# Strided slice by DMA alone: one queue for loads, one for stores, and single-batch copies beside them

## The chip, the cores and the metric

The kernel runs on one core of a Trainium2 chip. The metric is the device time of one execution in microseconds. Times are medians of several executions. The profile is of one execution, and its span (first to last instruction) is about 1.8 us shorter than the time of that execution. "GB/s" counts bytes that the core's 16 DMA engines moved; a byte copied from HBM to HBM counts once there, though HBM reads it and writes it.

## The reference

```python
batch, seq, dim = 32, 1024, 512          # float32; start, stop, stride = 0, 512, 2
def reference(x, start, stop, stride):
    return x[:, start:stop:stride, :].astype(np.float32)
```

Of each batch, rows 0, 2, 4 ... 510 are kept: 256 rows of 2 KB, 4 KB apart in the input and adjacent in the output. The output has 16.78 MB.

## The kernel before

Nothing is computed, so the kernel is only transfers. It sends half of the rows of a batch straight from HBM to HBM (a copy, issued by GpSimd) and the other half through SBUF (a load, later a store). The halves are the even and the odd kept rows. `apart` tells which half of batch b is copied directly, and it changes every two batches.

```python
def apart(b):
    return 1 - (b >> 1 & 1)

def two(t, b, step, parity):             # one half of two batches, step apart
    return t[b : b + step + 1 : step].rearrange("b (p two) d -> two p b d", two=2)[parity]
...
    src = x[:, start:stop:stride, :]
    held = [io.tile([P, 2, D], x.dtype, name=f"held{i}") for i in range(B // 2)]
    for g in range(0, B, EIGHT):
        for i, (b, step) in enumerate(((0, 5), (2, 5), (1, 3), (3, 3))):
            b += g
            at = g + 2 * i
            (sp, act)[i % 2].dma_start(held[at // 2], two(src, at, 1, 1 - apart(at)))       # load
            pool.dma_start(two(out, b, step, apart(b)), two(src, b, step, apart(b)))        # copy
    for b in range(B):
        to = out[b].rearrange("(p two) d -> two p d", two=2)[1 - apart(b)]
        sp.dma_start(to, held[b // 2][:, b % 2])                                            # store
```

All 16 loads and 16 copies come first, and SyncE (SP) issues all the stores behind its loads. Every pair of batches has its own SBUF tile, so no buffer is ever waited for.

Of the kernel before, what the change touches and what calls it, by code (L numbers as in the profile page):

```python
# [3 lines left out]

EIGHT = 8


def apart(b):


    return 1 - (b >> 1 & 1)


def two(t, b, step, parity):

    return t[b : b + step + 1 : step].rearrange("b (p two) d -> two p b d", two=2)[parity]


def kernel(tc, x, start, stop, stride, out):





    nc = tc.nc
    src = x[:, start:stop:stride, :]
    B, rows, D = out.shape
    P = rows // 2
    sp, act, pool = nc.sync, nc.scalar, nc.gpsimd
    with tc.tile_pool(name="io", bufs=1) as io:  # L30
        held = [io.tile([P, 2, D], x.dtype, name=f"held{i}") for i in range(B // 2)]
        for g in range(0, B, EIGHT):
            for i, (b, step) in enumerate(((0, 5), (2, 5), (1, 3), (3, 3))):
                b += g
                at = g + 2 * i
                (sp, act)[i % 2].dma_start(held[at // 2], two(src, at, 1, 1 - apart(at)))
                pool.dma_start(two(out, b, step, apart(b)), two(src, b, step, apart(b)))  # L37
        for b in range(B):
            to = out[b].rearrange("(p two) d -> two p d", two=2)[1 - apart(b)]
            sp.dma_start(to, held[b // 2][:, b % 2])  # L40


# [1 line left out]
_INS = ['x', 'start', 'stop', 'stride']  # L44
_OUTS = [((32, 256, 512), 'float32')]

_NUMBERS = {'start': 0, 'stop': 512, 'stride': 2}


def kernel(**inputs):  # L50
    import numpy as _np
    import concourse.bacc as _bacc
    import concourse.tile as _tile
    from concourse import mybir as _mybir
    from concourse.bass_utils import run_bass_kernel_spmd as _run

    nc = _bacc.Bacc("TRN2", target_bir_lowering=False, num_devices=1)  # L57
    arrays, args = {}, []
    for name in _INS:
        if name in _NUMBERS:  # L60
            args.append(_NUMBERS[name])
            continue
        a = _np.ascontiguousarray(inputs[name])
        if a.dtype.kind in "iu":
            a = a.astype(_np.int64)
        arrays[f"in_{name}_dram"] = a
        args.append(nc.dram_tensor(f"in_{name}_dram", a.shape, _mybir.dt.from_np(a.dtype), kind="ExternalInput").ap())
    for i, (shape, dtype) in enumerate(_OUTS):
        dt = _mybir.dt.from_np(_np.dtype(dtype))
        args.append(nc.dram_tensor(f"out_{i}_dram", shape, dt, kind="ExternalOutput").ap())  # L70
    with _tile.TileContext(nc) as tc:  # L71
        kernel(tc, *args)
    r = _run(nc, [arrays], core_ids=[0])
    got = tuple(r.results[0][f"out_{i}_dram"] for i in range(len(_OUTS)))
    return got[0]
```

## Time and profile before

| What | Value | From |
|---|---|---|
| time | 79.45 us median of 3 (79.29 to 79.64) | the runs |
| the profiled execution | 79.17 us, span 77.4 us | its result, the page |
| loads, copies, stores | 8.39 MB each | the page's queue rows and issues |
| mean rate of the DMA engines | 325 GB/s | the page |
| rate of HBM, read and written | 434 GB/s over the span | the page |

The prediction below shows the lines behind this. A share of 1 means that the times of the packets add up to the time of all 16 engines (it reaches 1.06 here, as packets overlap a little). The rate can still differ, because a packet can be held up while it is in progress. The packet records of the trace give each packet's start, length, size and queue.

### The profile page before, as it was taken

To read this page: it belongs to the slowest core of one execution; us is meant where nothing else is said; L and a number is where in the kernel's file an instruction comes from. 1 tells how busy PE (TensorE), PEld (TensorE's weight loads), DVE (VectorE), ACT (ScalarE), POOL (GpSimd) and SP (SyncE) were. 2 spreads that over 40 slices of the span, in tenths; PEclk is the share of its full clock that TensorE was granted. 3 is DMA by queue.
4 is the path that set the end of the run, shared out by engine and by line. 5 is a ranking of instruction groups with operands and counts; after the bars stand their busy time and mean duration, and the time that the engine had idled before them with its cause. 6 is when DMAs were issued, how large, how long until landed. Compare 5 with 4: busy or idle time off the path is not lost. (4 is left out here: it accounts for less than half of the span.)

```text
span 77.4 us, 113 instructions
## 1 busy us (share of the span) xinstructions
POOL 11.3 (15%) x20
## 2 busy tenths in 40 slices
POOL 4995003303023031130000000000000000000000
DMA  0799999999999999999999999999999999999960
GB/s 7 235 303 334 332 281 347 327 310 386 351 349 363 364 314 358 358 321 333 323 300 310 347 307 357 413 392 339 402 404 405 375 356 347 361 356 353 350 216 20
DMA packets 11264, 25.17 MB, mean 325 GB/s; under 512 B 1024, under 2 KB 1024, under 8 KB 11264
## 3 DMA queue, kind: packets, MB, share of 16 engines
q1 hardware_dynamic: 6784, 12.59, 48.1%
q0 software_dynamic: 2304, 8.39, 29.3%
q10 hardware_dynamic: 2176, 4.19, 17.7%
HBM read 16.78 MB, written 16.78 MB: 434 GB/s over the span
## 5 line engine op out<-in xcount | busy, mean ns | idle before, releaser
L37 POOL DMA_DIRECT2D out_dram<-in_x_dram x16 | 11.1, 696 | 22.6 <-DMA out_dram<-in_x_dram 21.8
L57 POOL MEMSET const-float32-0.0<- 128x1 f32 x1 | 0.1, 99 | 0.2 <-issue 0.2
L57 POOL MEMSET const-bfloat16-1.0<- 128x1 bf16 x1 | 0.1, 102 | 0.0
L57 POOL MEMSET const-uint8-127<- 128x1 uint8 x1 | 0.1, 100 | 0.0
L57 POOL MEMSET const-float32-1.0<- 128x1 f32 x1 | 0.1, 99 | 0.0
## 6 DMA issues: line engine op xcount, KB each, us to landing
out_dram<-in_x_dram POOLq DMA_DIRECT2D x16, 512.0 KB, 23.6
out_dram<-held SPq DMA_DIRECT2D x32, 256.0 KB, 6.1
held<-in_x_dram ACTq DMA_DIRECT2D x8, 512.0 KB, 22.9
held<-in_x_dram SPq DMA_DIRECT2D x8, 512.0 KB, 22.7
```

Source lines behind the costliest of these rows:

```text
L37: pool.dma_start(two(out, b, step, apart(b)), two(src, b, step, apart(b)))
L57: nc = _bacc.Bacc("TRN2", target_bir_lowering=False, num_devices=1)
```

## The change

The intent is to let reads and writes run side by side from early on. Loads go to SP, stores to ScalarE (ACT) four pairs of batches behind, and copies are cut to one batch each on GpSimd's queue.

```diff
-        for g in range(0, B, EIGHT):
-            for i, (b, step) in enumerate(((0, 5), (2, 5), (1, 3), (3, 3))):
-                b += g
-                at = g + 2 * i
-                (sp, act)[i % 2].dma_start(held[at // 2], two(src, at, 1, 1 - apart(at)))
-                pool.dma_start(two(out, b, step, apart(b)), two(src, b, step, apart(b)))
+        def load(queue, i):
+            queue.dma_start(held[i], two(src, 2 * i, 1, 1 - apart(2 * i)))
+
+        def store(queue, b):
+            queue.dma_start(one(out, b, 1 - apart(b)), held[b // 2][:, b % 2])
+
         for b in range(B):
-            to = out[b].rearrange("(p two) d -> two p d", two=2)[1 - apart(b)]
-            sp.dma_start(to, held[b // 2][:, b % 2])
+            nc.gpsimd.dma_start(one(out, b, apart(b)), one(src, b, apart(b)))
+        for i in range(AHEAD):                       # AHEAD = 4
+            load((sp, act)[i % 2], i)
+        for i in range(AHEAD, pairs):
+            load(sp, i)
+            for k in range(2):
+                store(act, 2 * (i - AHEAD) + k)
+        for b in range(B - 2 * AHEAD, B):
+            store((sp, act)[b % 2], b)
```

Here `one(t, b, parity)` is one half of one batch.

More of the change, by code (lines that the diff above doesn't have):

```diff
@@ L3 @@
 from concourse import mybir
-EIGHT = 8
+AHEAD = 4
 def apart(b):
@@ L28, with one @@
     P = rows // 2
-    sp, act, pool = nc.sync, nc.scalar, nc.gpsimd
+    sp, act = nc.sync, nc.scalar
+    pairs = B // 2
+    def one(t, b, parity):
+        return t[b].rearrange("(p two) d -> two p d", two=2)[parity]
     with tc.tile_pool(name="io", bufs=1) as io:
-        held = [io.tile([P, 2, D], x.dtype, name=f"held{i}") for i in range(B // 2)]
-        for g in range(0, B, EIGHT):
-            for i, (b, step) in enumerate(((0, 5), (2, 5), (1, 3), (3, 3))):
-                b += g
-                at = g + 2 * i
-                (sp, act)[i % 2].dma_start(held[at // 2], two(src, at, 1, 1 - apart(at)))
-                pool.dma_start(two(out, b, step, apart(b)), two(src, b, step, apart(b)))
-        for b in range(B):
-            to = out[b].rearrange("(p two) d -> two p d", two=2)[1 - apart(b)]
-            sp.dma_start(to, held[b // 2][:, b % 2])
+        held = [io.tile([P, 2, D], x.dtype, name=f"held{i}") for i in range(pairs)]
+        def load(queue, i):
+            queue.dma_start(held[i], two(src, 2 * i, 1, 1 - apart(2 * i)))
+        def store(queue, b):
+            queue.dma_start(one(out, b, 1 - apart(b)), held[b // 2][:, b % 2])
+        for b in range(B):
+            nc.gpsimd.dma_start(one(out, b, apart(b)), one(src, b, apart(b)))
[7 more added lines that the diff above has]
+            store((sp, act)[b % 2], b)
 _INS = ['x', 'start', 'stop', 'stride']
```

## The prediction

> **What bounds the kernel now.** The kernel computes nothing: 8.39 MB go from HBM to SBUF (loads), the same 8.39 MB from SBUF to HBM (stores), and the other half of the output, 8.39 MB, straight from HBM to HBM (copies). I first read the DMA rows of the page. They say whether the 16 DMA engines are idle (columns: 40 slices of 1.94 us).
>
> ```profile
> DMA  0799999999999999999999999999999999999960
> ...
> q1 hardware_dynamic: 6784, 12.59, 48.1%
> q0 software_dynamic: 2304, 8.39, 29.3%
> q10 hardware_dynamic: 2176, 4.19, 17.7%
> HBM read 16.78 MB, written 16.78 MB: 434 GB/s over the span
> ```
>
> They are not idle: busy at 90% or more from the third slice to the 38th. So no wait on a semaphore can be saved; time can only come from the two ends, or from packets that take less time per byte. The three rows below it are the queues (packets, MB, share): q1 belongs to SyncE (SP: 8 loads and all 32 stores), q10 to ScalarE (ACT: 8 loads), q0 to GpSimd (copies). The packets count out as follows: each transfer ends with 16 small ones, one for each engine, so q0 has 2304 - 16 x 16 = 2048 of data, 4,096 B each; q10 has 2176 - 8 x 16 = 2048, 2,048 B each; q1 has 6784 - 40 x 16 = 6144, also 2,048 B.
>
> Next, the rate by stage. The summed packet records show that SP's last load packet starts at 46.9 us, ACT's at 48.8, the last copy's at 55.4. With those borders I asked for the windows (columns: stretch, length, POOL busy, clock, DMA share, GB/s moved):
>
> ```profile
> 0.00:2.00 2.00, 0.93 (x5) 1.00 0.03 12
> 2.00:6.00 4.00, 4.00 (x7) 1.00 0.89 274
> 6.00:48.00 42.00, 6.36 (x10) 1.00 1.00 334
> 48.00:54.00 6.00, 0.00 (x0) 1.00 1.02 384
> 54.00:60.00 6.00, 0.00 (x0) 1.00 1.04 403
> 60.00:74.00 14.00, 0.00 (x0) 1.00 1.05 355
> 74.00:77.40 3.40, 0.00 (x0) 1.00 0.24 91
> ```
>
> The engines are equally busy throughout, and still move 334 GB/s in one stage and 384 to 403 in another. The stages are, in order: nothing yet; loads alone; loads beside copies; copies beside stores; stores almost alone (twice); the end. Splitting the same packet records by queue gives the mean time of a packet in each (ns; floor is the commonest value):
>
> ```
> stage     copy 4 KB   load 2 KB    store 2 KB
> floor        159          84           84
> 6-48 us      177       104 / 108        -
> 48-54        175           -            84
> 54-60         -            -            84
> 60-74         -            -            96
> ```
>
> So the costly stage is 6 to 48 us, where every packet in progress reads HBM: about one load packet in eleven is held up by hundreds of ns (the longest 972), and loads cost 25% over their floor. It takes 42 of the 77.4 us. Stores cannot start in it: those that are issued stand behind SP's remaining loads in the same queue.
>
> ```profile
> out_dram<-in_x_dram POOLq DMA_DIRECT2D x16, 512.0 KB, 23.6
> out_dram<-held SPq DMA_DIRECT2D x32, 256.0 KB, 6.1
> held<-in_x_dram ACTq DMA_DIRECT2D x8, 512.0 KB, 22.9
> held<-in_x_dram SPq DMA_DIRECT2D x8, 512.0 KB, 22.7
> ...
> SPq L40 <- DMA held<-in_x_dram: 22.0, 4, 6.5
> SPq L36 <- DMA held<-in_x_dram: 19.8, 4, 5.7
> SPq L40 <- DMA out_dram<-held: 12.9, 24, 2.2
> ```
>
> The first four (KB each, us from issue to landing) show deep queues: a load takes 22.7 us to land because about 4 MB stand in line. The others are SP's waits (total, times, longest). They fit eight transfers in flight on SP and ACT together and eight on GpSimd (POOL's 9th copy is the first to wait); the semaphores named in the trace are eight and eight too. As the engines stay full, these waits cost nothing now.
>
> **What the Trainium skill says.** "DMA: Bandwidth & Descriptors", section "Issuing engines are not separate DMA queues", says that transfers of all issuers run on the same 16 engines and that issuing from several saves only issue time. The trace agrees that more queues add no capacity: stores from one queue run at 403 GB/s, three queues of loads and copies at 334. The same page, "Queues, rings and completion order", says that an engine goes round robin between queues by packet. It agrees: in 6 to 48 us, q0, q1 and q10 move 161, 87 and 87 GB/s, close to 2:1:1, as 4 KB packets against 2 KB ones would. "HBM Reference", section "Specifications (TRN2)", puts a core streaming alone at about 425 GB/s, bounded by its DMA engines; the best stage here is 403. "Perfetto Trace Analysis", section "DMA Optimizations", suggests one issuing engine for inputs and another for outputs; the kernel before does not do so, and whether it pays here is what the change tests.
>
> **The change, part by part.**
> (1) Bytes: none removed. 25.17 MB pass the engines before and after.
> (2) Copies: 16 of 512 KB become 32 of 256 KB. Rows of two batches are no longer side by side in one transfer, so I expect packets of 2 KB: 32 x (128 + 16) = 4608 records. At the floor, two take 2 x 84 = 168 ns against 159: 9 ns for each 4 KB. Issuing costs POOL at most 32 x 0.69 us = 22 us, all beside other work. Eight in flight are now 2 MB instead of 4, some 16 us of work at a third of the engines: enough.
> (3) Order: stores have ACT's queue from the start, after two loads. The copies, SP's loads and ACT's stores then get equal shares (2 KB each), and have 8.39 MB each. Two thirds of the packet time reads HBM instead of all of it.
> (4) In flight: with eight lanes over loads and stores in program order, load i waits for the first store of pair i-7, and the second store of pair i-4 for load i-2. With loads some four pairs ahead, that leaves about three loads and two pairs of stores queued (1.5 and 1 MB). I expect no engine to starve.
>
> The sum. The closest stage of before to the new mix is 48 to 54 us: copies reading 250 GB/s beside stores, where a copy packet and a store packet took 175 + 84 = 259 ns for 6 KB and the engines moved 384 GB/s. With the 9 ns of (2) that is 384 x 259 / 268 = 371 GB/s. If stores cost 96 ns instead, as after 60 us, it is 384 x 259 / 280 = 355. I take 367, nearer the first, as 96 was seen only late in the store stage.
> - 0 to 2 us: start, as before.
> - 2 to 6: loads alone, 274 GB/s: 1.10 MB.
> - 6 to 11: loads and copies at 334, until ACT's two loads (1.05 MB, 0.49 of them moved by 6 us, the rest at 111 GB/s) have left its queue: 1.67 MB.
> - The remaining 25.17 - 2.77 = 22.40 MB at 367 GB/s: 61.0 us, to 72.0.
> - The end: before, the bytes would have been out at 74.0 + 0.31 MB / 355 GB/s = 74.9, and the span ended 2.5 later: 74.5.
> - Measured time less span: 79.45 - 77.40 = 2.05 us: 76.6.
>
> I go slightly lower, to 76.2, as the mix may reach 384 in part; that is 4% faster.
>
> **Rivals.** (a) Every read packet is held up as before whatever runs beside it: 105 for a load, about 105 for a 2 KB copy, 88 for a store, 298 ns per 6 KB, 330 GB/s; 22.40 MB take 67.9 us, total 83.4. For it: a copy took 175 in 48 to 54 us, hardly less than the 177 before. Against it: that mean comes from two bad microseconds; from 48 to 52 it was 160 or 161.
> (b) Reads are the only thing short (about 334 GB/s in the loads' stage), and at two thirds of the traffic packets run at their floor: 3 x 84 = 252 ns, 390 GB/s or a little more: 57.4 us, total 73.0. For it: the flat 84 and 160 in 48 to 52 us. Against it: loads held up even alone at 274.
> (c) The lanes couple loads to stores so that one queue runs dry in turn. The other queues would fill the engines, so it costs only at the end, if the copies are left alone: 1 to 2 us.
> (d) More queues and more traffic in both directions make HBM slower for all. Against it: 48 to 54 us carries 634 GB/s over HBM (250 read, 384 written), and the new mix would carry about 490.
>
> **Range and chances.** "Faster" needs under 77.86 us, 1.66 above my estimate, which means 359 GB/s in the mixed stage; 355 (stores at 96) lands within 2%, and rival (a) is slower. The evidence for the mix is 6 us long, so I keep a good part for those: 0.60 faster, 0.26 same, 0.14 slower; 72.0 to 80.2 us should hold it.
>
> **What would show it.** Right: q0 with 4608 packets; three near-equal queues from about 11 us on; windows there at 360 to 375 GB/s; load packets nearer 90 than 105 ns; DMA share at 1 to the end. Wrong: windows still near 334 with loads at 105 (rival a); near 390 (b); a DMA share under 0.95 in the middle or a long stretch at the end with one queue (c); store packets well over 96 ns (d).

## The result

The changed kernel took 82.19 us median (81.25 to 82.67, 4 runs), against 79.37 us (78.98 to 79.64) for the kernel before on the same chip. The ratio is 1.0319 with a 95% interval of 1.0214 to 1.0424: slower. One of the four runs counts as slow and is left out of the ratio. Ratios here are the mean time of one kernel's fast runs over that of the other's, so they are not quite the ratio of the medians quoted. The prediction was wrong: it said 76.2 us and faster.

The changed kernel's page, the rows of DMA share in 40 slices and of the queues (packets, MB, share):

```profile
DMA  0899999999999999999999999999999999999940
...
q0 software_dynamic: 2560, 8.39, 33.7%
q1 hardware_dynamic: 4384, 8.39, 31.9%
q10 hardware_dynamic: 4576, 8.39, 28.0%
HBM read 16.78 MB, written 16.78 MB: 418 GB/s over the span
```

The engines are as busy as before, and the queues now carry equal bytes. But q0 holds 2560 packets, not 4608: less 32 x 16 small ones, 2048 data packets, so copies still go in packets of 4 KB. Its share is the largest for the same bytes. As times, 33.7% of 80.2 us is 27.0 us of all 16 engines for the copies; before it was 29.3% of 77.4 us, 22.7 us.

The changed kernel's windows (columns as in the prediction). The first store packet starts at 13 us, the last copy packet at 63.6, the last load packet at 70.8:

```profile
0.00:2.00 2.00, 0.95 (x6) 1.00 0.09 8
2.00:6.00 4.00, 3.49 (x7) 1.00 0.91 279
6.00:12.00 6.00, 1.05 (x2) 1.00 0.99 278
12.00:58.00 46.00, 11.51 (x22) 1.00 1.01 339
58.00:64.00 6.00, 0.00 (x0) 1.00 1.01 348
64.00:76.00 12.00, 0.00 (x0) 1.00 0.96 353
76.00:80.20 4.20, 0.00 (x0) 1.00 0.28 109
```

The long stage with all three streams, 46 us, runs 339 GB/s. That is about the rate at which loads and copies ran before without stores (334). The fast stages of before, 384 and 403 GB/s, have no counterpart: the stores that ran in them are now inside the slow stage. By queue, 12 to 58 us moves 158 GB/s on q0, 93 on q1 and 88 on q10, so copies get nearly twice the share of the others and end first.

The waits of SP's queue in the changed kernel (total us, times, longest):

```profile
SPq L37 <- DMA out_dram<-held: 47.8, 9, 6.9
SPq L37 <- DMA held<-in_x_dram: 11.5, 1, 11.5
```

The loads (L37) now wait for stores that hold their lanes, as the prediction worked out. With a DMA share of 1.01 at the time, these 47.8 us cost almost nothing, in spite of their size.

### The profile page after: what moved, and what is told of

It reads as the page before. It is cut to its first block, busy times and chain, and to the rows that moved or that the text cites. A ratio compares the mean times of both kernels' runs of the same rounds, so it can differ in the third digit from the quotient of the medians.

```text
span 80.2 us, 134 instructions
## 1 busy us (share of the span) xinstructions
POOL 17.0 (21%) x36
## 3 DMA queue, kind: packets, MB, share of 16 engines
q0 software_dynamic: 2560, 8.39, 33.7%
## 4 chain that ended last, share of the span: by engine, by line
DMA 56%; POOL 5%; issue 3%; POOLq 1%; PEldq 0%
DMA out_dram<-in_x_dram 56%; POOL out_dram L43 5%; POOLq L82 1%; PEldq L82 0%
## 5 line engine op out<-in xcount | busy, mean ns | idle before, releaser
L43 POOL DMA_DIRECT2D out_dram<-in_x_dram x32 | 16.8, 527 | 34.9 <-DMA out_dram<-in_x_dram 34.1
```

The source lines that it names most:

```text
L43: nc.gpsimd.dma_start(one(out, b, apart(b)), one(src, b, apart(b)))
```

## Where the packet time goes

The commonest packet takes 84 ns (2 KB load or store) or 159 ns (4 KB copy) in every run. I call the excess over that "held up". Summed over all packets of a stream and divided by 16 engines, it is in us of full engine time. "Rest" is the span less the summed time of all packets: start, end, and engines without work (it comes out a little small where packets overlap). Each row is one profiled execution.

```
run                        loads   copies  stores   all packets   rest
before                      5.6     2.2     1.8        73.6        3.8
e9, before again            5.4     3.4     1.9        74.7        3.3
e12, neighbouring batches   6.0     2.8     2.1        74.8        3.2
e15, copies cut by rows     5.2     3.4     1.9        74.6        3.6
e17, stores reordered       5.9     2.5     1.9        74.2        3.5
e1, before + single copies  4.8     4.3     1.2        74.4        4.6
e16, e1 in another order    5.1     4.2     1.1        74.5        5.8
after                       4.4     6.4     0.2        75.1        5.2
e2, after + double copies   8.7     4.0     0.1        76.8        4.1
e14, e2 on both queues      7.6     4.3     1.4        77.2        3.9
e5, one-batch copies alone   -      5.0      -
e6, two-batch copies alone   -      6.0      -
e7, loads alone             4.2      -       -
e13, loads on one queue     4.1      -       -
e8, loads and stores        8.1      -      1.7
e11, contiguous loads       1.2      -       -
```

Loads and stores on one queue are told apart by the order in which their packets start, which is good to a few packets (rougher in e14, where they alternate on both queues). In the changed kernel it is the copies that are held up more than before, 6.4 us against 2.2; its loads are held up less, 4.4 against 5.6. The experiments below refer to this table.

## The experiments

18 kernels ran. Where a time is compared with the kernel before, it is that of the same job: 79.37 us for e1 to e4, 79.39 for e5 to e8, 79.72 for e9 to e12, 79.74 for e13 to e16 and 79.71 for e17 and e18. Ratios use fast runs alone (e1 is an exception, told there); a run over 1.5% above its kernel's fastest counts as slow. e5 to e9, e11 and e13 ran once, and their state is unknown.

**e1: the split of the copies alone.** The kernel before, with this edit (`one` as in the changed kernel):

```diff
-                pool.dma_start(two(out, b, step, apart(b)), two(src, b, step, apart(b)))
+                for c in (b, b + step):
+                    pool.dma_start(one(out, c), one(src, c))
```

> The kernel before with each two-batch copy of 512 KB cut into its two one-batch copies, in the same order; loads and stores untouched. Theory S (the shape of the copies costs the time: in the changed kernel a 4 KB copy packet took 206 ns at 12 to 58 us against 177 before): copy packets go from 177 to about 200 ns in the stage of loads and copies, and the time from 79.4 to 81.5 or more. Theory M (the mix of copies with loads and stores costs it, not the shape): copy packets stay at 173 to 181 ns and the time within 1% of before, 78.6 to 80.2 us.

81.69 us, ratio 1.0299 (1.0228 to 1.0369). Two of its four runs count as slow, 82.08 and 82.30, and the ratio fits only with them in it. The two fast runs, 80.79 and 81.29, have a mean of 81.04 against 79.49 for the kernel before: 1.95% more. So the split costs 2 to 3%. That is in theory S's direction, but its reason isn't quite right: copies are held up 2 us more than in before, loads and stores 1.4 us less, and the sum of all packets, 74.4 us, is the mean of the five kernels with two-batch copies (73.6 to 74.8). What differs is the rest, 4.6 us against 3.2 to 3.8. Windows of e1 show where a part of it lies; its last copy packet starts at 58.7 us:

```profile
58.00:64.00 6.00, 0.00 (x0) 1.00 0.96 368
66.00:70.00 4.00, 0.00 (x0) 1.00 1.04 362
74.00:76.00 2.00, 0.00 (x0) 1.00 0.65 227
```

In the kernel before, stores run at a share of 1.04 to 1.06 from 56 to 72 us. In e1 the share dips as the copies end, and then recovers. So some engines seem to be out of work for a while when others still have some; which ones, the trace can't show.

**e2: the split undone in the changed kernel.**

```diff
-        for b in range(B):
-            nc.gpsimd.dma_start(one(out, b, apart(b)), one(src, b, apart(b)))
+        for g in range(0, B, 8):
+            for b, step in ((0, 5), (2, 5), (1, 3), (3, 3)):
+                b += g
+                nc.gpsimd.dma_start(two(out, b, step, apart(b)), two(src, b, step, apart(b)))
```

> The changed kernel with the two-batch copies of the kernel before, in their old order; loads and stores as changed. Theory S: copy packets fall from 206 to about 177 ns, the stretch 12 to 58 us moves 355 to 375 GB/s and the time falls to 76 to 79 us. Theory M: copy packets stay above 200 ns and the time within 1.5% of the changed kernel, 81 to 83.4 us.

82.71 us, ratio to before 1.0385 (1.0333 to 1.0436): theory M's time. Copy packets fell only to 191 ns (theory M had them above 200), and loads rose from 101 to 118. The split alone costs 2 to 3%, the mix alone almost 4%, and both together 3.2%: the two don't add. Windows of e2:

```profile
12.00:48.00 36.00, 5.50 (x8) 1.00 1.01 331
48.00:58.00 10.00, 0.00 (x0) 1.00 1.02 341
```

A full share and a low rate: reads held up, not engines out of work.

**e3 and e4: one fixed half for the copies**, in the changed kernel (e3) and in the kernel before (e4).

```diff
-    return 1 - (b >> 1 & 1)
+    return 1
```

> The changed kernel with one fixed half for the copies: they always take the odd rows of each pair of rows, loads and stores always the even ones. Theory P (copies and loads that read, or copies and stores that write, rows of the same parity hold each other up, and the alternation lets them meet): they never meet now, so copy packets go to about 165 ns, loads under 90, and the time to 72 to 76 us. Theories S and M: no change, 81 to 83.4 us. A fourth outcome, slower than 84 us, would say that one stream needs the alternation to spread its own rows.

> The kernel before with the same fixed half. Theory P: copies and loads never share a parity, so the stage of loads and copies rises from 334 GB/s towards 390 and the time falls to 73 to 77 us. S and M: within 1% of before, 78.6 to 80.2 us. If a stream needs the alternation to spread its own rows, it is slower than 81 us.

88.45 us (ratio 1.1134) and 90.14 us (1.1308). Theory P falls: streams that never meet on one parity are slower. The stretch 12 to 48 us moves 281 and 257 GB/s. Which rows a stream takes when mattered more here than the schedule of the queues, and both kernels have the better of these two choices. With the fixed half, the changed schedule (e3) is even the faster of the two, and the intervals, 1.1072 to 1.1196 and 1.1233 to 1.1383, lie apart. So whether the change gains or loses depends on the rows that meet.

**e5 and e6: copies alone**, of one batch and of two (all loads and stores deleted, so the result is wrong).

> Wrong result on purpose: the 32 one-batch copies of the changed kernel and nothing else. Theory S (a one-batch copy is slow by its own shape): copy packets well above 159 ns alone, about 200, 320 GB/s. Theory I (the slow packets come from meeting other streams): 159 to 168 ns, 390 to 410 GB/s in the middle.

> Wrong result on purpose: the 16 two-batch copies of the kernel before and nothing else. S: packets at 159 to 168 ns, clearly faster than the one-batch copies alone. I: the same as the one-batch copies alone, within 3%.

34.19 and 34.79 us. Copy packets took 198 and 206 ns in the mean. Theory S had the one-batch number, but not the contrast that it stands on: the one-batch copy isn't slower than the two-batch one. Theory I falls as well: both are held up with nothing beside them, most of all at first (226 and 276 ns at 2 to 12 us). So what the split lost in e1 shows only beside the other streams. The engines weren't always full here (share 0.81 at 2 to 12 us in e5, 0.87 at 12 to 30 in e6), so this comparison is rough. Alone, the copies are held up 5.0 and 6.0 us, more than the 2.2 to 3.4 beside loads in the kernel before and its kin: fewer reads at a time did not mean less holding up here.

**e7: loads alone**, alternately on SP and ACT, with two stores at the end (wrong result). The edit deletes the copies and the other stores.

> Wrong result on purpose: the 16 loads alone, alternately from SP and ACT, and two stores at the end. If reads hold each other up whatever runs beside them (the loads' stage of before ran at 274 GB/s before the copies came, but that was the first 4 us): load packets stay near 105 ns, under 340 GB/s. If they need the copies beside them to be held up: 84 to 90 ns, 380 GB/s or more.

The windows (share and GB/s last):

```profile
2.00:6.00 4.00, 0.00 (x0) 1.00 0.94 284
6.00:12.00 6.00, 0.00 (x0) 1.00 0.97 297
12.00:20.00 8.00, 0.00 (x0) 1.00 1.02 333
20.00:28.00 8.00, 0.00 (x0) 1.00 0.99 347
```

Loads are held up with nothing beside them: 100 ns in the mean, falling from about 107 to 93.

**e8: the changed kernel without its copies** (wrong result).

> Wrong result on purpose: the changed kernel without its copies: loads on SP, their stores on ACT four pairs behind. If loads and stores disturb each other at HBM: loads near 105 ns, stores at 84 to 96, under 350 GB/s while both run with a DMA share of 1. If the copies are what disturbs: loads under 92 ns. If the eight lanes starve a queue, as the DMA share of 0.96 after the copies' end in the changed kernel hints: a share of 0.90 to 0.96 throughout.

58.7 us. The middle of it:

```profile
12.00:30.00 18.00, 0.00 (x0) 1.00 1.05 326
30.00:50.00 20.00, 0.00 (x0) 1.00 1.00 313
```

The share is 1, so lanes starve nothing. At 30 to 50 us a load takes 126 ns and a store 85 (the 123 of later expectations counts some stores on SP as loads). Loads are held up 8.1 us in all, nearly twice the 4.2 us of e7. It isn't always the loads that pay: at 12 to 20 us a load takes 95 ns and a store 112. But together they are held up 9.8 us, against 4.2 for the loads alone (e7) and 1.8 for stores in the kernel before. So loads and stores beside each other are held up more than apart, with no copy in the kernel. e8 has its loads on one queue and e7 on two, but loads alone on one queue are held up as in e7 (e13 below).

**e9: the kernel before, once more**, unchanged, for a second trace.

> The kernel before, unchanged, for a second trace of it. The prediction rested on its stage of copies beside stores, 384 GB/s over 6 us. If that stage is a property of the mix, it is 375 to 395 again. If it was luck (the split copies of e1 ran 340 GB/s in the same stretch), it lies elsewhere, between 300 and 400, while the stage of loads and copies stays within 3% of 334.

79.79 us. The stretch that the prediction leaned on, from e9's windows:

```profile
6.00:48.00 42.00, 6.36 (x10) 1.00 1.00 330
48.00:54.00 6.00, 0.00 (x0) 1.00 1.03 362
```

The long stage repeats to about 1% (334 before). The short one gives 362 for 384, outside the band set for a property of the mix. Kernels with two-batch copies gave 343 (e12), 349 (e15) and 370 (e17) there.

**e10: halves as first and second 128 rows**, in the kernel before.

```diff
-    return t[b : b + step + 1 : step].rearrange("b (p two) d -> two p b d", two=2)[parity]
+    return t[b : b + step + 1 : step].rearrange("b (two p) d -> two p b d", two=2)[parity]
```

(and likewise for the stores)

> The kernel before with the two halves of a batch taken as its first and second 128 output rows instead of its even and odd ones, so that a stream's rows follow one another at 4 KB in the input and without gaps in the output. Correct result. If the large step of 8 KB between a stream's rows is what holds the reads up: loads near 90 ns, the first stage at 360 to 390 GB/s, 70 to 76 us. If not: within 2% of before, 78 to 81 us, or slower.

89.46 us, ratio 1.1227. A miss: in this kernel, rows at 4 KB are slower than rows at 8 KB with alternating halves.

**e11: loads of contiguous rows**, alone as in e7 (wrong result).

```diff
-            queue.dma_start(held[i], two(src, 2 * i, 1, 1 - apart(2 * i)))
+            queue.dma_start(held[i], x[2 * i : 2 * i + 2, :P].rearrange("b p d -> p b d"))
```

> Wrong result on purpose: the loads alone of e7, but each batch's 128 rows taken one after the other in memory instead of every fourth. In e7 a load packet took 106 ns at 2 to 12 us and 94 at 20 to 28. If the strided rows hold the reads up: 84 to 88 ns and 385 to 405 GB/s from the start. If any read of this size is held up: 95 to 108 ns as in e7.

```profile
2.00:6.00 4.00, 0.00 (x0) 1.00 0.99 359
6.00:12.00 6.00, 0.00 (x0) 1.00 1.05 393
12.00:20.00 8.00, 0.00 (x0) 1.00 1.05 387
```

This is the clearest result. The bytes, packets and queues are those of e7, and only the addresses differ: loads are held up 1.2 us in place of 4.2. So most of what holds these loads up lies in the addresses: rows 8 KB apart instead of 2 KB. The 8 KB are this kernel's choice, as the task asks for rows 4 KB apart; loads at 4 KB were not run alone. It is one run of each.

**e12: copies of neighbouring batches**, in the kernel before.

```diff
-            for i, (b, step) in enumerate(((0, 5), (2, 5), (1, 3), (3, 3))):
+            for i, (b, step) in enumerate(((0, 1), (2, 1), (4, 1), (6, 1))):
```

> The kernel before, with copies of two neighbouring batches (0 and 1, 2 and 3, ...) instead of 0 and 5, 2 and 7 and so on: still 512 KB each. It tells what the split of e1 lost. If it is the size in flight or the packet of two batches: as before, 78.6 to 80.2 us. If it is the distance of the two batches that are read at once: as e1, 81 to 82.5 us.

79.72 us, ratio 0.9994 (0.9948 to 1.004). The distance of the two batches made no difference.

**e13: e7's loads on one queue** (`load(sp, i)`; wrong result).

> Wrong result on purpose: the loads alone of e7, but all on SP's queue, as the changed kernel has them, instead of alternately on SP and ACT. Loads of neighbouring pairs take opposite parities, so two queues read both parities at once and one queue reads one. If that matters (theory Q: loads on one queue are held up more; the loads of e8 took 123 ns on one queue at 30 to 50 us): 110 to 125 ns and under 310 GB/s in the middle. If not: as e7, 94 to 106 ns, 330 to 350 GB/s.

36.8 us against 34.11, but the load packets took 100.2 ns in the mean, exactly as in e7. Theory Q falls. The time is lost at the end, where the rate falls from 25 us on, to about 100 GB/s and less in the last 3 us of loads; it seems that not all engines have work left.

**e14: e2 with loads on both queues.**

```diff
-            load(sp, i)
+            load((sp, act)[i % 2], i)
             for k in range(2):
-                store(act, 2 * (i - AHEAD) + k)
+                store((act, sp)[i % 2], 2 * (i - AHEAD) + k)
```

> The changed kernel with the two-batch copies of e2 and, in addition, its loads alternately on SP and ACT, each pair's stores on the other queue. Theory Q: load packets fall from the 118 ns of e2 to about 104 and the time to 79 to 80.5 us. If it is the mix with stores that holds the reads up, not the queue: as e2, 82 to 83 us.

82.39 us, ratio 1.033 (1.0271 to 1.039): as e2, with load packets of 114 ns. Spreading the loads over both queues is no cure. Together with e8 this leaves the running of stores beside reads, and the rows that then meet.

**e15: two-batch copies cut by rows** in the kernel before: as many and as small as e1's.

```diff
-                pool.dma_start(two(out, b, step, apart(b)), two(src, b, step, apart(b)))
+                for h in (0, P // 2):
+                    s = slice(h, h + P // 2)
+                    pool.dma_start(two(out, b, step, apart(b))[s], two(src, b, step, apart(b))[s])
```

> The kernel before with each two-batch copy cut by rows instead of by batches: two copies of 256 KB, each with 64 rows of both batches. As in e1, 32 copies and 2 MB in flight; unlike e1, a 4 KB packet still takes one row of each of two batches. If e1 lost its 2.3 us to the smaller amount in flight or to the number of copies: 81 to 82.5 us. If to the packet of two rows of one batch: as before, 79 to 80.3 us.

79.92 us, ratio 1.003 (0.9967 to 1.0094). So e1 lost neither to 256 KB transfers nor to 2 MB in flight. What is left is that each transfer copies one batch.

**e16: e1 with the rows of a copy in another order**, meant to deal them out to the engines one by one. In e1's `one`:

```diff
-        return t[c].rearrange("(p two) d -> two p d", two=2)[apart(c)]
+        return t[c].rearrange("(j e two) d -> two e j d", e=16, two=2)[apart(c)]
```

> e1 (one-batch copies in the kernel before) with the rows dealt out to the 16 engines one by one[...]. Correct result. If the engines hold each other up through their spacing: copy packets under 175 ns, and the time under 80 us. If the spacing is not it: within 1.5% of e1, 80.5 to 82.9 us.

81.83 us, ratio 1.0255 (1.0187 to 1.0324): as e1, though unclear at 2%. This order of rows doesn't help. That it spaces the engines as meant is not shown, as the trace doesn't give a packet's engine.

**e17: stores in order of parity**, an attempt at a better kernel.

```diff
-        for b in range(B):
+        for b in sorted(range(B), key=apart, reverse=True):
```

> An attempt to beat both kernels: the kernel before with its stores in another order, first all batches whose stored rows are even, then all whose stored rows are odd. In the kernel before the last stores alone ran 355 GB/s with packets of 96 ns; where the stored rows never change parity (e4) and the stores were alone they ran 405 at 84. If the alternation of parity is what slows the stores: about 5 MB at 405 instead of 355 saves 14.0 - 12.3 = 1.7 us, 77.4 to 78.5 us, packets of 84 to 88 ns after 60 us. If not: within 1% of before.

79.55 us, ratio 0.9984 (0.9962 to 1.0005): a miss. Stores took 94 to 96 ns from 60 us on as before, so the alternation isn't what slows them. In e4, 66 to 80 us ran 401 GB/s, and in e18 below every store ran at 84 ns. Why, stays open.

**e18: copies of four batches** with parity changing every four, on top of e17; SP and ACT load pairs of opposite parity:

```diff
-    return 1 - (b >> 1 & 1)
+    return 1 - (b >> 2 & 1)
...
+            for i, b in enumerate((g, g + 4, g + 2, g + 6)):
+                (sp, act)[i % 2].dma_start(held[b // 2], two(src, b, 1, 1 - apart(b)))
+            for b in (g, g + 4):
+                pool.dma_start(four(out, b, apart(b)), four(src, b, apart(b)))
```

> e17 with the parity changing every four batches and copies of four neighbouring batches, 1 MB each, with SP's and ACT's loads still at opposite parities. If more batches side by side in a copy make the engines more even, as two did against one (e1): the engines end closer together and the time is 0.5 to 1.5 us under e17. If two batches are all that is to be had: within 1% of e17.

90.49 us, ratio 1.1344. Copies took 240 ns in the mean, so the question of the even end drowned in held-up reads. It changed the order of the loads, the parity and the size of the copies at once and doesn't tell which did it. No version beat the kernel before.

## Why the prediction was wrong

**What bounds the kernel: right.** The DMA engines stayed full, no wait mattered, and the first 6 us went as said (279 GB/s for 274). The reading that packets are held up in the stage of reads was right too. The conclusion that fewer reads at a time would be held up less was not. (A small slip in rival (d): at 48 to 54 us HBM had 257 GB/s read and 377 written, not 250 and 384, as 7 GB/s of ACT's loads were still running.)

**Part (2), packets of the copies: wrong, small.** They stayed at 4 KB. The Trainium skill, "DMA: Bandwidth & Descriptors", section "SWDGE vs HWDGE vs iDMA", gives packets of preferably up to 4096 B; the 2048 data packets of 4,096 B fit that for two rows of one batch as for one row of two. The 9 ns charged for it were not due; without them the estimate would have been further off.

**Part (3), equal shares: wrong, as a consequence of that.** With packets of 4 KB beside 2 KB, copies took 158 GB/s against 93 and 88 and ended at 63.6 us, and loads and stores ran on without them. Up to 64 us the share is 1, so the unequal shares cost nothing there. After 64 us the DMA share is 0.96, which is about 0.5 us of idle engines in 12 us.

**Part (4), the lanes: right.** SP's loads waited 47.8 us in all for stores, at a DMA share of 1.01. e8 has the same lanes, no copies to fill in, and a share of 1.00.

**The sum.** Term by term against the profiled execution of 82.0 us: the stretch from 6 us took 6 us instead of 5 for its 1.67 MB (278 GB/s instead of 334): +1.0. The remaining 22.36 MB were moved by about 77.3 us (0.45 MB were left at 76 us, 1.3 us at 353 GB/s), so 65.3 us instead of 61.0, or 342 GB/s in the mean instead of 367: +4.3. The end took 2.9 us instead of 2.5: +0.4. The difference of time and span was 1.8 instead of 2.05: -0.25 (the profiled execution of the kernel before took 79.17 us, so 1.8 was due there too; the prediction took the median of other executions). That is 76.6 + 5.45 = 82.05; the last step of the prediction, from 76.6 down to 76.2 for hope of 384 GB/s, adds 0.4 to the miss.

So the step that failed is "The closest stage of before to the new mix is 48 to 54 us". It failed in two ways. First, the 384 GB/s was a lucky stretch of 6 us: the unchanged kernel gave 362 in its second trace (e9). Second, and more, it was taken to show that reads are held up less beside writes. In the prediction's terms, a copy of 2 KB, a load and a store should have taken 268 ns together. At 12 to 58 us they took 103 (half of 206) + 98 + 84 = 285. The stores were at their floor as assumed; the copies, 175 at 48 to 54 us before, were not held up less but more. The other runs show the same: loads are held up 4.2 us alone (e7), 8.1 beside stores (e8); all reads 7.8 to 8.8 in the kernel before and its close kin, 12.7 in e2 with the same copies and the stores beside. Which reads pay differs: the loads in e2 (8.7), the copies in the changed kernel (6.4). Loads by themselves are held up mostly through their addresses (e11: 1.2 us on contiguous rows), and no schedule tried here took that away.

**The rivals.** Rival (a), every read packet held up whatever runs beside it, came nearest, at 330 GB/s and 83.4 us against 342 and 82.19, and its packet times too, 105 for a load and 105 for 2 KB of a copy. That is partly luck: it took a load's 105 for the copy because it expected split packets. My argument against it rested on the four good microseconds from 48 to 52. Rival (b), reads as the only thing short, is refuted by the mixed stage itself: from 12 to 58 us loads and copies read about 250 GB/s, far under the 334 of before, and yet copies took 206 ns and loads 98. In e8 only 139 GB/s were read at 30 to 50 us, and loads took 126. Rival (c) is small, as said. Rival (d), HBM slower for all, isn't so for stores: they took 84.7 ns in the mean in the changed kernel, against 91.1 before; but in e8 they took 112 at 12 to 20 us.

**Why slower, and not merely no faster.** Against the five two-batch kernels at the top of the table (before, e9, e12, e15, e17), the changed kernel has reads (loads and copies) held up 10.8 us instead of 7.8 to 8.8, stores 0.2 instead of 1.8 to 2.1, and a rest of 5.2 instead of 3.2 to 3.8. The middle of each gives roughly +2.5, -1.8 and +1.7, which is 2.4 us; the spans differ by 2.3 (80.2 against a mean of 77.9). The first comes mostly with the mix: reads are held up 12.7 us in e2 and 11.9 in e14, but 9.1 in e1 and 9.3 in e16, which have the split and not the mix. The gain on stores is real, but is given back there. The third goes with copying one batch at a time (e1 and e16 have 4.6 and 5.8; e2, without the split, 4.1).

**Open.** Why one-batch copies leave the engines uneven is not settled: it is not their size, number or amount in flight (e15), another order of rows doesn't help (e16), and alone they are no slower (e5, e6). Why the two losses don't add is only described by the table. Whether stores slow any read or only reads at these addresses is not tested: loads of contiguous rows beside stores were not run, and e3 against e4 shows that the rows decide even the sign of the change. Why the strided rows are slow, no run here can show.

## What to carry to other kernels

When all DMA engines are full, ask why a packet is slow before rearranging who issues what: a run of the same transfers on contiguous addresses tells in one look whether the addresses are the cause. Don't take the rate of a new mix from a short stretch of the old one; take a second trace first, and run each stream alone and in pairs. Running reads beside writes is no gain in itself here: what the stores saved, the loads and copies lost. With other rows (e3 against e4) the same change gained 1.5%, so measure a schedule together with its addresses.

## What the Trainium skill lacked or had wrong

- "DMA: Bandwidth & Descriptors", section "Latency and other measured facts", tells of slow copies only for row pitches from 512 KiB up. Here loads of 2 KB rows at 8 KB, two batches 2 MB apart, ran 297 GB/s at 6 to 12 us, and contiguous ones 393 (e7, e11). Which half of the rows a stream takes when moved the whole kernel from 79.4 to 90.1 us (e4).
- No page that I found tells what stores do to loads beside them in the same DMA engines: the loads' mean packet went from 100 ns alone to 116 (e7, e8).
- "Perfetto Trace Analysis", section "DMA Optimizations", says that separate issuing engines for inputs and outputs may make sense, especially with loops or control flow. Here it made no difference: ratio to before 1.0385 with them apart (e2) and 1.033 with them mixed (e14), their intervals overlapping.
- The same section advises larger sizes, with examples from 2 KB to 8 KB, which no run here tests. It says nothing of how a large transfer is cut: halving the copies to 256 KB by rows cost nothing (e15, 1.003), and cutting them by batches cost 2 to 3% (e1).
